# Issuing the background loads of an encoder kernel from ScalarE's queue

## The chip, the cores and the metric

The kernel runs on one core of a Trainium2 chip. The metric is the device time of one execution in microseconds; the time before is the median of three runs. One further execution was recorded by the hardware profiler, and all rows of the trace come from that one.

## The reference, cut to what matters

An encoder layer of width 1024 is applied to 512 prompt tokens and 2048 sample tokens, all in float32:

```python
h = rmsnorm(x, norm_pre)
z = h @ w_in
pool_u, pool_g, q, k, v, attn_g, merge = jnp.split(z, cuts, axis=-1)
pooled = multiscale_pool(pool_u)
pb = jnp.einsum('bsgc,gcd->bsgd', pooled, w_pool_group).reshape(B, S, POOL_WIDTH)
pb = pb * pool_scale * jax.nn.silu(pool_g)
q, k = rope(q, pos), rope(k, pos)
ab = windowed_attention(q, k, v, attn_sink) * jax.nn.silu(attn_g)
gates = jax.nn.sigmoid(merge)
m = gate_pool * (pb @ w_pool_proj) + gate_attn * (ab @ w_attn_proj)
out = x + rmsnorm(m @ w_out, norm_post)
```

## The kernel before, in words

Every float32 operand is split into a rounded high part and a low remainder (`hi_lo`, lines 106 to 108: ScalarE (ACT) copies the high part, VectorE (DVE) subtracts it), and every product takes three matmuls (`mm3`, lines 144 to 147). The kernel has two phases.

Phase 1 (`phase1`, to about 1180 us) forms the input projection in three blocks of 768, 896 and 896 tokens (`BLOCKS`). In each block, 26 pairs of weight columns go through a seven-product Strassen scheme (`pair_steps`, order M1, M6, M2, M5, M7, M3, M4). One product, an item, is 12 matmuls on a weight tile `w` that ACT and DVE have split; seven such tiles are in flight (`TILES = 7`). Between the items the results leave PSUM: ACT copies M1 (line 460) and M2 (`post.first`, lines 499 and 513), DVE adds the others (lines 464, 474, 442). M2 is accumulated on M1's bank, two items later, so the ACT copy of M1 must be done by then. The raw weights `R`, `A21` and the stored sums `Q` come by DMA on SyncE's queue (SP), in lines 402, 406 and 414.

Beside these, phase 1 runs background tasks, each a load and, later in the program, a form step (`task`):

- `stats_load` (line 253) loads rows of x for the next block, and ACT squares them (line 260): 28 loads.
- `later_load` (line 355) loads the transposed x of the next block, `later_form` normalizes it on DVE (line 367) and stores pieces `t` from GpSimd's queue (POOL): 32 loads.
- `late_load` (lines 679 and 680) loads back parts of the pooling branch put aside in block 0, `late_pool` finishes them (ACT's sigmoid in line 688) and stores `pb`: 20 loads.
- `split_load` (line 849) loads halves of `w_attn_proj`, `split_form` splits them on ACT and DVE and stores both parts: 16 loads in phase 1. Phase 2 uses the same function for other weights.
- `fold` multiplies the pooling groups into the pooling columns of w_in; `raw_load` (line 181) brings its operands, items 0 to 3 at the start and items 4 to 7 (12 loads) from about 113 us on. Its results go to memory as `wpool`.

All of these loads write tiles of one tag, `h` (`htile`), of which there are four buffers. The temporaries of the forms, the tiles of the stores `t`, `v`, `wpool`, `w_ap` and `pb`, and the operand pieces fetched in line 384 take buffers of the same tag, in turn. A load may go out when the former owner of its buffer is done with it, which for stored tiles means that the store has landed.

Phase 2 (from about 1180 us) is attention, the two branch projections and the output projection. None of its loads is touched.

The order on TensorE (PE) is the program's own. On the other engines and queues the framework lays down one fixed order in advance, by the order of the program and by when it reckons that an instruction can start; on the chip each engine then works strictly in that order, and a wait holds all that is behind it.

```python
        def raw_load(src, n):
            raw = (htile, utile)[n % 2 if n < 4 else 0]()
            nc.sync.dma_start(raw, src)
            return raw
```

Of the kernel before, what the change touches and what calls it, by code (L numbers as in the profile page):

```python
# [47 lines left out]
def encoder(ctx, tc, a, out):  # L48
    nc = tc.nc
    V, A, G, T = nc.vector, nc.scalar, nc.gpsimd, nc.tensor  # L50
# [8 lines left out]
    def psum(tag):  # L59
        return ps.tile([128, 512], F32, tag=tag, bufs=PS[tag], name="ps_" + tag)  # L60
# [4 lines left out]
    def htile():  # L65
        return sb.tile([128, 512], F32, tag="h", bufs=NH, name="h")
# [22 lines left out]
    def wtile():  # L89
        return sb.tile([128, 2, 512], F32R, tag="w", bufs=NW, name="w")  # L90

    def load(shape, src, tag):
        t = const.tile(shape, F32, tag=tag, name=tag)
        nc.sync.dma_start(t, src)
        return t
# [4 lines left out]
    def store(dst, src):  # L100
        G.dma_start(dst.bitcast(F32), src.bitcast(F32))

    def scratch(name, shape, dt=F32):
        return dr.tile(shape, dt, tag=name, bufs=1, name=name)

    def hi_lo(hi, lo, src):
        A.copy(hi, src)  # L107
        V.tensor_sub(lo, src, hi.bitcast(F32))  # L108
# [17 lines left out]
    rawu = [scratch(f"rawu{f}", [128, n0 + 24]) for f in range(8)]  # L126
    rawg = [scratch(f"rawg{f}", [128, n0]) for f in range(8)]
# [16 lines left out]
    def mm3(o, xs, ys, start, stop, more=False):  # L144
        T.matmul(o, lhsT=xs[0], rhs=ys[0], start=start, stop=False, skip_group_check=more)  # L145
        T.matmul(o, lhsT=xs[0], rhs=ys[1], start=False, stop=False, skip_group_check=more)  # L146
        T.matmul(o, lhsT=xs[1], rhs=ys[0], start=False, stop=stop, skip_group_check=more)  # L147
# [28 lines left out]
    def fold():  # L176
        steps, fetches = [], []

        def raw_load(src, n):
            raw = (htile, utile)[n % 2 if n < 4 else 0]()  # L180
            nc.sync.dma_start(raw, src)
            return raw

        def split(raw):
            w = wtile()
            hi_lo(w[:, 0, :], w[:, 1, :], raw)
            return w

        for g in range(4):
            for half in range(2):  # L190
                hs = slice(half * 512, (half + 1) * 512)
                n, raws = 2 * g + half, []

                def fetch(g=g, hs=hs, n=n, raws=raws):
                    raws += [raw_load(x, n) for x in (a["w_pool_group"][g], a["wu_t"][2 * g, :, hs], a["wu_t"][2 * g + 1, :, hs])]

                def make(n=n, raws=raws, fetch=fetch):
                    if n < 4:
                        fetch()
                    return [split(x) for x in raws]  # L200
                fetches.append(fetch)
                it = Item(make, 3)
                st = {}
                for i in range(4):
                    def f(it=it, st=st, i=i, g=g, half=half):
                        if i % 2 == 0:
                            st["p"] = psum("t")
                        o = st["p"][:, i % 2 * 256:(i % 2 + 1) * 256]
                        for c in range(2):
                            u = [it.w[1 + c][:, e, i * 128:(i + 1) * 128] for e in range(2)]  # L210
                            mm3(o, u, [it.w[0][:, e, c * 256:(c + 1) * 256] for e in range(2)], c == 0, c == 1)
                        if i % 2 == 1:
                            t = htile()
                            A.copy(t, st["p"])
                            tv = t.rearrange("p (r c) -> p r c", r=2)
                            k0 = half * 4 + i - 1
                            for c in range(2):
                                dst = wp[2 * g + c][:, k0 * 128:(k0 + 2) * 128].rearrange("p (r c) -> p r c", r=2)
                                store(dst, tv[:, :, c * 128:(c + 1) * 128])
                    steps.append((it, f))  # L220
        return steps, fetches
# [24 lines left out]
    def stats_load(s, ts):  # L246
        if s not in ssqs:
            ssqs[s] = sb.tile([128, 16], F32, tag="ssq", bufs=2, name="ssq")
        res = []
        for t in ts:  # L250
            for j in range(2):
                res.append((t, j, htile()))
                nc.sync.dma_start(res[-1][2], a["x"][t * 128:(t + 1) * 128, j * 512:(j + 1) * 512])
        return res

    def stats_sum(s, xs):
# [91 lines left out]
    def later_load(s, k, c):  # L348

        a_, b = BLOCKS[s]  # L350
        w = (b - a_) // 2
        res = []
        for j in range(2):
            t = htile()[:, 0:w].rearrange("p (i t) -> p i t", i=2)
            nc.sync.dma_start(t, a["xt"][k + 4 * j, :, a_:b].rearrange("p (i t) -> p i t", i=2)[:, :, c * w // 2:(c + 1) * w // 2])
            res.append(t)
        return res

# [317 lines left out]
    def late_load(f, j):  # L676
        m0, m1, g0, g1 = LATE[j][:4]
        u, g = htile(), htile()
        nc.sync.dma_start(u[:, 0:m1 - m0 + 16], rawu[f][:, m0:m1 + 16])
        nc.sync.dma_start(g[:, 0:g1 - g0], rawg[f][:, g0:g1])  # L680
        return u, g

    def late_pool(f, j, ug):
# [11 lines left out]
    def phase1():  # L695
# [29 lines left out]
        def src(i):  # L725
            return [(0, 2048, a["w_h"][i])]
# [6 lines left out]
        for s in range(len(BLOCKS)):  # L733
            specs = [(0, src(0), Rope(s, kd)), (1, src(1), Values(s))]
            for kv in range(NKV):
                g = {
                    "q": (2 + kv, src(2 + kv), Rope(s, qd[kv])),
                    "ag": (6 + kv, src(6 + kv), Silu(s, (2 * kv, 2 * kv + 1))),
                    "ga": (10 + kv, src(10 + kv), Gate(s, gad, (2 * kv, 2 * kv + 1))),
                    "gp": (14 + kv, src(14 + kv), Gate(s, gpd, (2 * kv, 2 * kv + 1))),  # L740
                }
# [19 lines left out]
        def hook(s, i, j, f):  # L761
            hooks.setdefault((s, i, j), []).append(f)
# [4 lines left out]
        def task(s, load, form):  # L767
            box = {}
            tasks[s].append((lambda: box.update(x=load()), lambda: form(box["x"])))

        for s in range(len(BLOCKS)):
            hook(s, 1, 6, lambda s=s: load_rope(s, "rope_q"))
            for (i, j), f in zip(((2, 2), (2, 4), (3, 0), (3, 3)), posts[NPAIR * s + 1].tr_steps()):
                hook(s, i, j, f)
            if s + 1 == len(BLOCKS):
                continue
            t0, t1 = BLOCKS[s + 1][0] // 128, BLOCKS[s + 1][1] // 128
            for t in range(t0, t1, 2):
                ts = range(t, min(t + 2, t1))

                def stats(x, s=s, last=t + 2 >= t1):
                    stats_sum(s + 1, x)
                    if last:
                        rstd(s + 1)
                task(s, lambda s=s, ts=ts: stats_load(s + 1, ts), stats)
            for k in range(4):
                for c in range(2):
                    def form(x, s=s, k=k, c=c):
                        if k + c == 0:
                            prep_r(s + 1)  # L790
                        later_form(s + 1, k, c, x)
                    task(s, lambda s=s, k=k, c=c: later_load(s + 1, k, c), form)
            hook(s, NPAIR - 3, 6, lambda s=s: fetch_operand(s + 1, XOP[ORDER[0]]))
            for j, r in enumerate(ORDER):
                hook(s, NPAIR - 1, j, lambda r=r: put_operand(XOP[r]))
                if j < 6:
                    hook(s, NPAIR - 1, j, lambda s=s, r=ORDER[j + 1]: fetch_operand(s + 1, XOP[r]))

        for i in range(2 * NLATE):
            f, j = i // 2, i % 2  # L800
            task(1 if i < LATE1 else 2, lambda f=f, j=j: late_load(f, j), lambda x, f=f, j=j: late_pool(f, j, x))
        ap_keys = [k for k in swp if k[0] == "w_ap"]
        for u in range(0, 16, 2):
            task(2, lambda u=u: [split_load(k) for k in ap_keys[u:u + 2]], lambda x: [split_form(*y) for y in x])
        hook(0, 3, 0, lambda: nc.sync.dma_start(cst["mask"], a["mask"]))
        for j in range(5):
            hook(0, 1, j, form_next)
# [7 lines left out]
        for s in range(len(BLOCKS)):  # L815
# [9 lines left out]
            n = len(tasks[s])  # L825
            for k, (begin, form) in enumerate(tasks[s]):
                t = t0 + (t1 - t0) * k / n
# [14 lines left out]
                    prog.append((None, fold_raws[i + 1]))  # L842
        return prog

    def split_load(key):

        h = htile()
        n, u, j = key
        nc.sync.dma_start(h, a[n][u, j] if n == "w_out" else a[n][u, :, j * 512:(j + 1) * 512])
        return h, swp[key]  # L850

    def split_form(h, dst):
        t = htile()
        hi, lo = t.bitcast(F32R), h.bitcast(F32R)
        hi_lo(hi, lo, h)
        for e, x in enumerate((hi, lo)):
            store(dst[:, e, :], x)
# [419 lines left out]
```

## Time and profile before

| | |
|---|---|
| runs | 2423.81, 2428.3, 2431.71 us; median 2428.3 |
| profiled execution | 2437.32 us, of which the span from first to last instruction is 2435.5 us |
| granted TensorE clock, mean | 0.983 of full speed |
| busy over the span | PE 96%, DVE 73%, ACT 47%, POOL 19% |

Two levels of time are seen here: the device time of a run, and the span in the trace, which is 1.8 us shorter than the device time of the same execution. The busy shares are means over two phases with different work, so the stretch from 60 to 1180 us, in which all loads of the change lie, has to be read by itself. "SPq" is SyncE's DMA queue; waits put down to it are times in which its next DMA was held.

### The profile page before, as it was taken

Reading aid. Unit: us, or ns where it says so; the run is one execution under the profiler, and the core shown is the slowest. Engines: PE = TensorE matmul, PEld = TensorE weight load, DVE = VectorE, ACT = ScalarE, POOL = GpSimd, SP = SyncE. Lnnn points to the kernel's source line nnn. Section 1 sums busy time; section 2 is a strip of 40 time slices with the busy share of each in tenths; the row PEclk is TensorE's granted clock in tenths of the full one; section 3 lists DMA queues with packets and bytes.
Section 4 is the critical chain, followed back from the end, with each engine's and each line's share of the span. In section 5 each row is a group of like instructions: output and inputs, shape, how many; then the busy total and the mean of one; then the engine's idle time right before and its main releaser. Section 6 shows DMA issues by size and latency. Waiting matters only on the chain.

```text
span 2435.5 us, 34771 instructions
## 1 busy us (share of the span) xinstructions
PE 2328.3 (96%) x11680; PEld 2070.4 (85%) x11680; DVE 1770.1 (73%) x3451; ACT 1149.8 (47%) x2511; POOL 458.4 (19%) x962
## 2 busy tenths in 40 slices
PE   5999999999999999999999889999999999999998
PEld 5899999898998999988899767787788788888887
DVE  7967789875777687777667667895788478578632
ACT  6355443545434345434443356674566366456411
POOL 2232233221222110323211111111110111021011
PEclk8999999999999999999999999999999999999999
DMA  6587786767577556757755597889788788877784
GB/s 234 184 274 248 253 276 224 280 212 236 182 236 245 163 172 243 250 201 257 258 170 171 194 318 224 267 254 319 274 268 265 271 262 251 278 261 239 258 290 174
DMA packets 197043, 586.83 MB, mean 241 GB/s; under 512 B 27265, under 2 KB 46209, under 8 KB 186881
## 3 DMA queue, kind: packets, MB, share of 16 engines
q1 hardware_dynamic: 152288, 406.26, 51.5%
q0 software_dynamic: 44576, 178.36, 19.9%
q8 instruction: 92, 1.51, 0.3%
q14 instruction: 87, 0.70, 0.1%
HBM read 406.19 MB, written 178.32 MB: 240 GB/s over the span
## 4 chain that ended last, share of the span: by engine, by line
PE 38%; DMA 5%; DVE 4%; ACT 2%; issue 1%; POOL 0%; SPq 0%; POOLq 0%; ACTq 0%; DVEq 0%
PE ps_g L146 6%; PE ps_g L145 6%; PE ps_g L147 6%; PE ps_t L1115 3%; PE ps_s L147 2%; PE ps_s L145 2%; PE ps_s L146 2%; DMA h<-pb 2%; PE ps_o L1131 2%; PE ps_o L1130 2%; DMA h<-ab 2%; PE ps_s L1083 2%; PE ps_s L1084 2%; DVE ps_s L1089 1%; DVE Q L108 1%
## 5 line engine op out<-in xcount | busy, mean ns | idle before, releaser
L145 PE MATMUL ps_g<-arena,w 128*128 128x512 f32 (+2 forms) x1264 | 494.6, 391 | 15.2 <-ACT arena L107 7.5
L146 PE MATMUL ps_g<-arena,w 128*128 128x512 f32 (+2 forms) x1264 | 479.2, 379 | 0.5 <-DVE arena L108 0.5
L147 PE MATMUL ps_g<-arena,w 128*128 128x512 f32 (+2 forms) x1264 | 477.8, 378 | 0.1
L145 PE MATMUL ps_s<-arena,w 128*128 128x448 f32 (+1 forms) x1248 | 448.7, 360 | 24.2 <-DVE u L474 9.3
L146 PE MATMUL ps_s<-arena,w 128*128 128x448 f32 (+1 forms) x1248 | 447.2, 358 | 3.2 <-DVE arena L108 3.1
L147 PE MATMUL ps_s<-arena,w 128*128 128x448 f32 (+1 forms) x1248 | 446.5, 358 | 1.5 <-DVE w L108 1.4
L107 ACT CAST w<-Q 128x512 fp32r<-128x512 f32 x312 | 190.1, 618 | 237.9 <-PE ps_s L147 177.8
L145 PEld LDWEIGHTS ps_g<-arena,w 128*128 128x128 f32 x1264 | 240.8, 190 | 38.0 <-ACT arena L107 10.3
L145 PEld LDWEIGHTS ps_s<-arena,w 128*128 128x128 f32 x1248 | 236.5, 190 | 42.6 <-DVE z L442 7.4
L147 PEld LDWEIGHTS ps_g<-arena,w 128*128 128x128 f32 x1264 | 240.2, 190 | 35.6 <-DVE w L108 0.4
L146 PEld LDWEIGHTS ps_g<-arena,w 128*128 128x128 f32 x1264 | 241.2, 191 | 21.8 <-DVE arena L108 2.6
L146 PEld LDWEIGHTS ps_s<-arena,w 128*128 128x128 f32 x1248 | 236.4, 189 | 17.7 <-DVE arena L108 5.6
L147 PEld LDWEIGHTS ps_s<-arena,w 128*128 128x128 f32 x1248 | 236.8, 190 | 15.1 <-DVE w L108 2.9
L108 DVE TENSOR_TENSOR w<-Q,w 128x512 fp32r<-128x512 f32 x312 | 212.4, 688 | 36.8 <-ACT w L107 32.1
L1091 ACT ACTIVATE R<-ps_s,nm 128x384 f32<-128x384 f32 (+1 forms) x320 | 179.7, 562 | 108.6 <-DVE nm L1089 99.5
L108 DVE TENSOR_TENSOR w<-R,w 128x512 fp32r<-128x512 f32 x234 | 160.6, 689 | 84.6 <-ACT w L107 82.9
L1089 DVE CUSTOM_DVE_ANT_0 ps_s<-ps_s,mask,nsink 128x384 f32<-128x384 f32 (+1 forms) x320 | 188.6, 593 | 17.3 <-PE ps_s L1084 15.7
L107 ACT CAST w<-R 128x512 fp32r<-128x512 f32 x234 | 143.7, 620 | 93.9 <-PE ps_s L147 48.9
L108 DVE TENSOR_TENSOR Q<-ps_t,Q 128x512 fp32r<-128x512 f32 x224 | 153.6, 689 | 38.9 <-ACT Q L107 36.1
L108 DVE TENSOR_TENSOR arena<-h,arena 128x512 fp32r<-128x512 f32 (+2 forms) x140 | 89.9, 658 | 107.8 <-ACT arena L107 107.2
L1115 PE MATMUL ps_t<-ident,R 128*128 128x128 f32 x896 | 140.3, 278 | 19.7 <-DVE R L1100 10.8
L107 ACT CAST Q<-ps_t 128x512 fp32r<-128x512 f32 x224 | 130.8, 584 | 44.7 <-PE ps_t L1115 22.0
(226 smaller groups left out, 4154.6 us busy)
## 6 DMA issues: line engine op xcount, KB each, us to landing
Q<-sw SPq DMA_DIRECT2D x52, 1024.0 KB, 6.0
R<-in_w_h SPq DMA_DIRECT2D x54, 768.0 KB, 6.0
w<-w_ap SPq DMA_DIRECT2D x80, 512.0 KB, 4.8
w<-w_pp SPq DMA_DIRECT2D x64, 512.0 KB, 5.4
w<-w_out SPq DMA_DIRECT2D x56, 512.0 KB, 4.9
sw<-Q POOLq DMA_DIRECT2D x26, 1024.0 KB, 5.7
arena<-q SPq DMA_DIRECT2D x20, 1024.0 KB, 7.4
q<-z POOLq DMA_DIRECT2D x128, 112.0 KB, 2.7
```

What stands on the lines that cost most here:

```text
L107: A.copy(hi, src)
L108: V.tensor_sub(lo, src, hi.bitcast(F32))
L145: T.matmul(o, lhsT=xs[0], rhs=ys[0], start=start, stop=False, skip_group_check=more)
L146: T.matmul(o, lhsT=xs[0], rhs=ys[1], start=False, stop=False, skip_group_check=more)
L147: T.matmul(o, lhsT=xs[1], rhs=ys[0], start=False, stop=stop, skip_group_check=more)
L1083: T.matmul(s, lhsT=q, rhs=st["kh"][:, kc], start=True, stop=False)
L1084: T.matmul(s, lhsT=q, rhs=st["kl"][:, kc], start=False, stop=True)
L1089: V.tensor_tensor_reduce(s, s, mask[:, kb0 * 128:kb1 * 128], -1.0, nsink[:, H:H + 1], ALU.add, ALU.min, nm[:, h:h + 1])
L1091: A.activation(P[:, 0:nk], s, AF.Exp, bias=nm[:, h:h + 1], scale=-1.0, accum_out=l[:, h:h + 1])
L1115: T.transpose(tp[:, h * 128:(h + 1) * 128], pr[h][:, i * 128:(i + 1) * 128], cst["ident"])
L1130: T.matmul(o, lhsT=v, rhs=pts[i][:, 0, :], start=i == 0, stop=False)
L1131: T.matmul(o, lhsT=v, rhs=pts[i][:, 1, :], start=False, stop=i == kb1 - kb0 - 1)
```

## The change

Five `dma_start` calls go from `nc.sync` to `A`, which is `nc.scalar`: the loads of fold items 4 to 7, of `stats_load`, `later_load` and `late_load`, and those of `split_load` where a background task calls it. What is loaded, the buffers and the order in the program stay.

```diff
         def raw_load(src, n):
             raw = (htile, utile)[n % 2 if n < 4 else 0]()
-            nc.sync.dma_start(raw, src)
+            (A if n >= 4 else nc.sync).dma_start(raw, src)
             return raw
...
                 res.append((t, j, htile()))
-                nc.sync.dma_start(res[-1][2], a["x"][t * 128:(t + 1) * 128, j * 512:(j + 1) * 512])
+                A.dma_start(res[-1][2], a["x"][t * 128:(t + 1) * 128, j * 512:(j + 1) * 512])
...
             t = htile()[:, 0:w].rearrange("p (i t) -> p i t", i=2)
-            nc.sync.dma_start(t, a["xt"][k + 4 * j, :, a_:b].rearrange("p (i t) -> p i t", i=2)[:, :, c * w // 2:(c + 1) * w // 2])
+            A.dma_start(t, a["xt"][k + 4 * j, :, a_:b].rearrange("p (i t) -> p i t", i=2)[:, :, c * w // 2:(c + 1) * w // 2])
...
         u, g = htile(), htile()
-        nc.sync.dma_start(u[:, 0:m1 - m0 + 16], rawu[f][:, m0:m1 + 16])
-        nc.sync.dma_start(g[:, 0:g1 - g0], rawg[f][:, g0:g1])
+        A.dma_start(u[:, 0:m1 - m0 + 16], rawu[f][:, m0:m1 + 16])
+        A.dma_start(g[:, 0:g1 - g0], rawg[f][:, g0:g1])
...
-            task(2, lambda u=u: [split_load(k) for k in ap_keys[u:u + 2]], lambda x: [split_form(*y) for y in x])
+            task(2, lambda u=u: [split_load(k, A) for k in ap_keys[u:u + 2]], lambda x: [split_form(*y) for y in x])
...
-    def split_load(key):
+    def split_load(key, queue=nc.sync):
...
-        nc.sync.dma_start(h, a[n][u, j] if n == "w_out" else a[n][u, :, j * 512:(j + 1) * 512])
+        queue.dma_start(h, a[n][u, j] if n == "w_out" else a[n][u, :, j * 512:(j + 1) * 512])
         return h, swp[key]
```

## Rows read from the trace of the kernel before

**Rows 1.** The profile's first part: busy us and share of the span, by engine.

```profile
PE 2328.3 (96%) x11680; PEld 2070.4 (85%) x11680; DVE 1770.1 (73%) x3451; ACT 1149.8 (47%) x2511; POOL 458.4 (19%) x962
```

**Rows 2.** Windows: stretch, length, busy us by engine, granted clock, DMA share, GB/s.

```profile
60.00:1180.00 1120.00, 1086.24 (x5635) 1023.27 (x5634) 852.94 (x1443) 484.81 (x894) 278.62 (x524) 0.99 0.68 232
860.00:1080.00 220.00, 220.00 (x1088) 202.10 (x1087) 170.16 (x275) 97.54 (x176) 45.63 (x93) 1.00 0.62 212
1080.00:1180.00 100.00, 93.26 (x454) 85.77 (x453) 66.18 (x109) 42.22 (x75) 31.97 (x63) 0.98 0.80 275
```

**Rows 3.** Waits of PE, 60 to 1180 us: us in total, times, longest us.

```profile
PE ps_s L145 <- DVE u L474: 7.0, 5, 2.7
PE ps_s L145 <- DVE z L442: 6.4, 3, 2.5
PE ps_t L145 <- ACT w L107: 5.2, 2, 4.5
PE ps_g L145 <- ACT s L460: 3.6, 1, 3.6
...
PE ps_t L581 <- DVE h L108: 0.4, 1, 0.4
```

**Rows 4.** Waits of SyncE's DMA queue, 60 to 1180 us.

```profile
SPq L402 <- DVE w L108: 213.9, 48, 28.9
...
SPq L355 <- DMA t<-h: 78.2, 23, 13.0
...
SPq L849 <- DMA w_ap<-h: 37.2, 12, 8.6
...
SPq L253 <- ACT h L260: 19.7, 12, 4.1
...
SPq L849 <- DVE w L108: 0.2, 1, 0.2
```

**Rows 5.** Issue of the loads in lines 355 and 679: ns min/median/max, first and last start.

```profile
L355 SPq DMA_DIRECT2D h<-in_xt x32: 367/378/517, 208.5 to 733.4; - x32
L355 SPq EVENT_SEMAPHORE  x30: 17/284/10552, 207.9 to 732.5; - x30
...
L679 SPq DMA_DIRECT2D h<-rawu  x10: 319/320/388, 744.7 to 1068.1; - x10
```

**Rows 6.** Waits of ACT that a DMA ended, 60 to 1180 us.

```profile
ACT h L107 <- DMA h<-in_w_ap: 27.1, 7, 5.1
ACT h L688 <- DMA h<-rawg: 25.9, 7, 10.6
...
ACT h L107 <- DMA w_ap<-h: 8.9, 4, 3.5
...
ACT w L107 <- DMA Q<-sw: 7.6, 4, 4.5
ACT w L107 <- DMA R<-in_w_h: 6.6, 2, 5.5
...
ACT h L688 <- DMA v<-h: 5.1, 1, 5.1
...
ACT h L107 <- DMA pb<-h: 3.4, 1, 3.4
...
ACT L533 <- DMA q<-z: 0.3, 1, 0.3
```

**Rows 7.** The same waits of ACT, 860 to 1080 us alone.

```profile
ACT h L688 <- DMA h<-rawg: 11.2, 4, 4.9
...
ACT z L499 <- DMA k<-z: 0.9, 1, 0.9
```

**Rows 8.** Timeline near 746 us: start, us, engine, what; in brackets the idle time before.

```profile
749.98 0.53 ACT L688 ACTIVATE h<-h 128x392 f32<-128x392 f32 x1 [10.60 <-DMA h<-rawg]
...
741.61 0.69 DVE L367 SCALAR_TENSOR_TENSOR h<-h,gpre,rbc 128x448 f32<-128x448 f32 x1 [6.67 <-DMA h<-in_xt]
...
746.02 0.47 PE L145 MATMUL ps_s<-arena,w 128*128 128x448 f32 x1 [2.55 <-DVE z L442]
```

## The prediction

> **What bounds the kernel now.** I read the busy shares first, then the stretch in which the change acts, then the waits of PE in it, and last the waits of the queues and of ACT. PE is busy for 2328.3 of 2435.5 us, 96% [rows 1]: TensorE is the bound, and all that another engine or queue can give or take is PE's idle time. All loads that the change moves start between 113 and 1180 us, so I cut out 60 to 1180 us. There PE is busy for 1086.24 of 1120 us, idle for 33.8 [rows 2]. This is the whole purse: no relief in this stretch can give back more than 33.8 us, 1.4% of the time. The ten rows of PE's waits there sum to 33.5 us, from 7.0 down to 0.4 [rows 3], and none names a DMA: PE waits for evictions by DVE and ACT, and for two weight tiles in the fold (5.2 us). A late load reaches PE only through ACT or DVE standing still.
>
> How well does PE bear a standing ACT? In 60 to 1180 us ACT waits 156.9 us for DMAs (15 rows, 27.1 down to 0.3 [rows 6]). In 860 to 1080 us it waits 31.3 us for them (six rows, 11.2 down to 0.9 [rows 7]) and PE loses nothing, 220.00 of 220 us [rows 2]. In 1080 to 1180 us, where the loads of w_attn_proj lie, it waits 39.4 us for those loads and for stores that give back `h` buffers (27.1, 8.9 and 3.4 [rows 6]; all three fall in this stretch), and PE loses 6.74 of 100 us [rows 2]. So one us of ACT standing costs PE between 0 and 6.74 / 39.4 = 0.17 us. I take 0.17 as the price, since that stretch holds the very loads in question.
>
> **The change part by part.** It moves 108 loads: 12 of the fold, 28 of x, 32 of transposed x, 20 of the late pooling, 16 of w_attn_proj. No byte, buffer or compute instruction is added or taken.
>
> *Issue.* On SP one issue takes 320 ns (line 679) to 378 ns (line 355) [rows 5]; 108 of them are 35 to 41 us, I take 37, off SP and onto ACT. ACT has no DMA issue in this trace. ACT is idle for 635 of 1120 us [rows 2], and that idle time is the cover. The ends for PE are 0 and 37 × 0.17 = 6 us; I take 2, because most of these loads will stand in front of an ACT instruction that has to wait anyway. If the cover were gone, the 37 us would be paid at up to one for one.
>
> *Waits for a buffer.* A load is held until its `h` buffer is free. On SP, the six lines moved were held for 291 us in this stretch (30 rows, 78.2 down to 0.2 [rows 4]), 52 of these holds, 192 us, ending with the landing of a store. This is what moves to ACT, and behind it stand the casts of weight tiles and the copies of M1 and M2 that PE needs. The ends are 0 (ACT comes to each load after its buffer is free) and 291 us. SP has little else to do and arrives early, so its holds overstate ACT's. The nearest row is ACT's own use of such buffers: of 26 allocations of an `h` tile that ACT writes first (16 in the split of w_attn_proj, 10 in the late pooling), six waited for a store, 8.9 + 3.4 + 5.1 = 17.4 us [rows 6], 0.67 us for each. The 28 loads of x are mostly freed by ACT's own squares (19.7 us of SP's holds [rows 4]), which ACT itself has done before, so they cost nothing. That leaves 80 loads × 0.67 = 54 us. Half of it I count as spent already: near 746 us ACT stood for 10.60 us in front of the sigmoid, because the load that it waited for was itself held for a buffer [rows 8]. With the load on ACT, the wait moves to the load and the wait for the landing shrinks. So 27 us are new, × 0.17 = 4.6 us. The ends are 0 and 291 × 0.17 = 49 us.
>
> *What it gives.* On SP, weight loads in lines 402, 406 and 414 no longer stand behind a held background load. What those weights cost now is small: ACT waited 6.6 us for R and 7.6 us for Q [rows 6], 14.2 × 0.17 = 2.4 us for PE; I take 3 with the few DVE waits of the kind. SP's own holds in line 402, 213.9 us [rows 4], are waits for R buffers to come free, and stay. The ends are 0 and 11 us (worked out under the first rival).
>
> The row with the longest hold shows the mechanism: before a load in line 355 the queue's semaphore instruction lasted up to 10552 ns [rows 5], and the next DMA of that queue came after. The Trainium skill, page "DMA: Bandwidth & Descriptors", section "Anatomy of one DMA", says that a DMA's semaphore wait is done by the issuing sequencer before dispatch, not by the DMA engines; this row agrees, and taken with all of SP's holds it would give the upper end, about 2428 + 49 = 2477 us.
>
> *Sum.* 2 + 4.6 − 3 = +3.6 us. The profiled execution took 2437.32 us, span 2435.5 and 1.8 around it, and would become 2440.9; it stands 9 us above the median of the three runs, so I put the same +3.6 on that: 2428.3 + 3.6 = **2432 us**. A change under 0.3% (7.3 us) cannot be told from none here. My forecast is therefore no change that can be told, with a lean to slower; its own range is 2421 to 2436.
>
> **The rivals.**
> *Faster: the background loads stop queueing on SP.* In the SP order a background load also stands behind held weight loads, and lands late; the consumers then stand, DVE for 6.67 us near 742 us, after which PE lost 2.55 us [rows 8]. If the loads go out sooner, PE can win back 2.55 us here, the 5.2 us of the fold's weight tiles and the 3.6 us in front of the copy of M1 [rows 3]: 11 us, so 2417 us. For it: SP is held for 213.9 us in line 402 [rows 4]. Against it: the 291 us of holds are at the loads themselves, which had reached the head of their queue, so a buffer and not the queue was what they lacked.
>
> *Slower: ACT held in front of a PSUM copy.* The place is a load that ACT reaches before its buffer is free, with the copy of M1 (line 460) or a cast behind it. The single wait of 3.6 us for that copy [rows 3] came right after ACT had waited 3.4 us for a store to free a buffer [rows 6]. PE does one item between M1 and M2, and the wait decides once ACT is held longer than that item lasts. Without the halving and without cover, 54 + 37 = 91 us × 0.17 = 15 us: 2443 us. For it: 52 of SP's holds ended with a store, 3.7 us each on average. Against it: ACT stood 10.60 us near 746 us and PE's loss there is put down to DVE [rows 8].
>
> *Much slower: all holds carried over*, 291 + 37 = 328 us × 0.17 = 56 us, 2484 us; ACT would have to reach every load as early as SP did, while most of its casts are paced by PE.
>
> *The change frees nothing on SP*: the loads keep the same gates and share the same DMA engines, whose mean share in this stretch is 0.68 [rows 2]. Then the credit of 3 us falls away, 2435 us. The Trainium skill, same page, section "Issuing engines are not separate DMA queues", says that DMAs interleave on the same engines whoever issues them and that only issue time is saved; nothing in this trace contradicts it, and the sum by it would be 2435 us, inside the forecast.
>
> **How the numbers follow.** The forecast of no telling change, with the last rival inside it, has 0.42; faster 0.25; slower at some 2443 us 0.28; much slower 0.05. Moving loads between queues also lays the orders of both queues down anew, which can shift single PE waits of 1 to 4 us [rows 3] either way, so I give the faster side its quarter though its mechanism is weakly borne out. The range goes from 2414, just past the faster rival, to 2456, between the two slower ones; that leaves out some 0.1 on each side.
>
> **What would show it.** In the changed kernel's profile: 108 DMA issues on ACT's queue, of 0.3 to 0.4 us; ACT waits at the moved lines that a store ended, 25 to 90 us in sum; the waits for landing in lines 688 and 107 smaller than before; PE's idle time in 60 to 1180 us between 30 and 42 us. The forecast is wrong to the slow side if PE's waits for the copies in lines 460 and 499 come to more than 10 us, and wrong to the fast side if PE's idle time there falls under 27 us. If the time moves while PE's idle time in this stretch stays, the cause is not one that I name.

## The result and the profile after

The changed kernel takes 2460.06 us, the median of six runs (2451.81 to 2471.18); the kernel before, run beside it, 2429.12 us (2423.81 to 2431.71, six runs). The ratio is 1.0123 [1.0099, 1.0147]: slower by 1.2%, some 31 us, and 4 us above the upper end of the range. The profiled execution of the changed kernel took 2455.05 us, with a span of 2453.3 us; the one before took 2437.32 us. The two traces that can be compared thus lie 17.7 us apart, and the rest of the 31 us is the place of each within its runs: the one before stood 8 us above its median, this one 5 us below.

The first part of the changed kernel's profile (compare [rows 1]):

```profile
PE 2326.8 (95%) x11680; PEld 2073.7 (85%) x11680; DVE 1768.3 (72%) x3451; ACT 1151.6 (47%) x2511; POOL 461.9 (19%) x962
```

No engine has more work. PE was busy 2328.3 us and is busy 2326.8; what was added is idle time. The same windows as in [rows 2], and two more that cut the stretch in halves:

```profile
60.00:1180.00 1120.00, 1066.67 (x5524) 1010.42 (x5524) 839.88 (x1423) 475.78 (x877) 276.58 (x515) 0.98 0.67 226
860.00:1080.00 220.00, 218.99 (x1100) 204.69 (x1099) 169.41 (x273) 99.34 (x176) 43.16 (x88) 1.00 0.63 213
1080.00:1180.00 100.00, 92.11 (x439) 84.17 (x438) 70.46 (x114) 40.69 (x71) 29.68 (x60) 0.97 0.72 241
...
60.00:740.00 680.00, 643.83 (x3449) 618.66 (x3449) 514.72 (x896) 290.96 (x554) 176.76 (x314) 0.97 0.69 233
740.00:1200.00 460.00, 437.46 (x2139) 404.48 (x2138) 333.78 (x543) 192.90 (x339) 104.71 (x210) 0.98 0.65 219
```

In 60 to 1180 us PE is idle for 53.3 us, where it was 33.8: 19.6 us more, which is all of the 17.7 us between the two profiled executions. In the two halves, the same windows of the kernel before read:

```profile
60.00:740.00 680.00, 656.80 (x3535) 630.53 (x3534) 524.32 (x914) 299.26 (x567) 179.19 (x321) 0.98 0.70 237
740.00:1200.00 460.00, 447.01 (x2188) 408.59 (x2187) 345.30 (x554) 194.90 (x344) 102.05 (x208) 1.00 0.66 224
```

PE loses 13.0 us more in the first half and 9.6 us more in the second. The stretch 1080 to 1180 us, from which the forecast took its price, lost 1.2 us more. The moved loads end near 1190 us; phase 1 itself does not end at 1180 us: its last additions come near 1390 us in the trace before and near 1415 us in this one. Who keeps PE waiting is in its waits, 60 to 1180 us, of the changed kernel (us in total, times, longest; twelve rows that sum to 53.2 us, against ten with 33.5):

```profile
PE ps_s L145 <- DVE u L474: 24.8, 10, 4.6
PE ps_s L145 <- DVE z L442: 6.7, 2, 3.9
PE ps_t L145 <- ACT w L107: 4.5, 2, 2.4
PE ps_g L145 <- ACT s L460: 3.8, 4, 2.3
PE ps_g L145 <- ACT w L107: 3.6, 1, 3.6
```

Beside [rows 3] one row has clearly grown: DVE's PSUM addition in line 474, from 7.0 to 24.8 us. The copy of M1 in line 460 cost PE 3.6 us and costs 3.8. Yet DVE has no more to do, so it must itself have been kept waiting: its longest row of waits, for ACT's casts of weight tiles, grew by 25.8 us (60 to 1200 us, before and then after):

```profile
DVE w L108 <- ACT w L107: 102.1, 76, 5.7
DVE w L108 <- ACT w L107: 127.9, 86, 9.1
```

The waits of ACT, 60 to 1200 us, of the changed kernel:

```profile
ACT w L107 <- DMA t<-h: 40.8, 5, 11.0
ACT h L260 <- DMA h<-in_x: 25.9, 10, 6.8
...
ACT h L688 <- DMA h<-rawg: 20.3, 8, 7.0
...
ACT h L107 <- DMA h<-in_w_ap: 15.7, 8, 5.1
...
ACT s L460 <- DMA w_ap<-h: 13.0, 3, 6.1
...
ACT w L107 <- DVE h L369: 8.3, 2, 4.3
ACT s L460 <- DMA v<-h: 8.2, 2, 4.6
...
ACT w L107 <- DMA pb<-h: 5.0, 1, 5.0
```

A cast of a weight tile (line 107) reads no tile of a store, and neither does the copy of M1. That a store `t<-h` ended 40.8 us of idle time in front of casts means that a load stood between: ACT was held at the load until that store gave back its `h` buffer, and the cast went next. Added up, ACT's waits that a store of an `h` tile ended were 17.4 us in six [rows 6] and are 86.3 us in 19. Waits that ended when DVE or POOL had read the `h` tile of a form, as in the row with line 369, come to 20.0 us more and are absent before. In turn the waits for the landing of the loads moved (x, `rawg`, `w_ap`, the fold's operands) shrank from 100.8 to 75.7 us.

The timeline of the changed kernel near 403 us shows the chain from the hold to PE (start, us, engine, what; in brackets the idle time before):

```profile
393.92 1.34 POOL L101 DMA_DIRECT2D t<-h  x2
...
402.13 0.97 ACTq L355 DMA_DIRECT2D h<-in_xt  x2
...
403.20 0.62 ACT L107 CAST w<-Q 128x512 fp32r<-128x512 f32 x1 [8.95 <-DMA t<-h]
...
403.86 0.69 DVE L108 TENSOR_TENSOR w<-Q,w 128x512 fp32r<-128x512 f32 x1 [4.18 <-ACT w L107]
...
409.07 0.55 DVE L474 TENSOR_TENSOR u<-ps_s,s 128x384 f32<-128x384 f32 x1
...
409.77 0.41 PE L145 MATMUL ps_s<-arena,w 128*128 128x384 f32 x1 [1.69 <-DVE u L474]
```

Two stores of `t` are issued from 393.92 on and land at 402.06 and 402.66. ACT's queue stands in front of the first load from 393.64 to 402.09; ACT, through with its last cast at 394.25, sends the two loads from 402.13 on and computes again at 403.20. DVE stands for 4.18 us in front of the low part of that weight tile, then works through what has piled up, and its addition for PE comes at 409.07, too late by 1.69 us. No instruction on this chain waits for the data of the load that ACT sent.

### The profile page after: what moved, and what is told of

Same layout as the page of the kernel before. It is cut to its first block, busy times and chain, and to the rows that moved or that the text cites. A ratio compares the mean times of both kernels' runs of the same rounds, so it can differ in the third digit from the quotient of the medians.

```text
span 2453.3 us, 34691 instructions
## 1 busy us (share of the span) xinstructions
PE 2326.8 (95%) x11680; PEld 2073.7 (85%) x11680; DVE 1768.3 (72%) x3451; ACT 1151.6 (47%) x2511; POOL 461.9 (19%) x962
## 3 DMA queue, kind: packets, MB, share of 16 engines
q0 software_dynamic: 44576, 178.36, 19.6%
## 4 chain that ended last, share of the span: by engine, by line
PE 39%; DMA 4%; DVE 4%; issue 2%; ACT 2%; POOL 1%; SPq 0%; POOLq 0%; ACTq 0%; DVEq 0%
PE ps_g L146 6%; PE ps_g L145 6%; PE ps_g L147 6%; PE ps_t L1115 3%; PE ps_s L145 3%; PE ps_s L147 3%; PE ps_s L146 3%; DMA h<-ab 2%; PE ps_o L1131 2%; PE ps_o L1130 2%; PE ps_s L1084 1%; PE ps_s L1083 1%; DVE ps_s L1089 1%; DVE Q L108 1%; DMA h<-pb 1%
## 5 line engine op out<-in xcount | busy, mean ns | idle before, releaser
L145 PE MATMUL ps_s<-arena,w 128*128 128x448 f32 (+1 forms) x1248 | 452.1, 362 | 44.1 <-DVE u L474 29.8
L145 PEld LDWEIGHTS ps_s<-arena,w 128*128 128x128 f32 x1248 | 239.0, 192 | 62.8 <-issue 19.5
L146 PEld LDWEIGHTS ps_s<-arena,w 128*128 128x128 f32 x1248 | 239.3, 192 | 17.1 <-DVE arena L108 6.4
L147 PEld LDWEIGHTS ps_s<-arena,w 128*128 128x128 f32 x1248 | 239.7, 192 | 15.0 <-DVE w L108 3.8
```

## The experiments

Three theories were set against each other. H (hold): ACT, held in order at loads whose buffer a store has yet to free, delays DVE and then PE. I (issue): what costs is the issuing itself, 108 DMA instructions of 0.33 to 0.37 us each on an engine that computes. O (order): what costs is the order of ACT's and DVE's instructions, which the framework lays down anew whenever loads leave SyncE's queue, whatever is held.

**Parts alone.** Each kernel moves some of the loads of the diff and leaves the rest on SP. The kernel before, run beside them, took 2431.95 us.

```diff
 # the part with transposed x only (32 loads)
-            nc.sync.dma_start(t, a["xt"][k + 4 * j, :, a_:b]...)
+            A.dma_start(t, a["xt"][k + 4 * j, :, a_:b]...)
 # the part with x and the fold only (28 and 12 loads)
-            nc.sync.dma_start(raw, src)
+            (A if n >= 4 else nc.sync).dma_start(raw, src)
-                nc.sync.dma_start(res[-1][2], a["x"]...)
+                A.dma_start(res[-1][2], a["x"]...)
 # the part with the late pooling and w_attn_proj only (20 and 16 loads)
-        nc.sync.dma_start(u[:, 0:m1 - m0 + 16], rawu[f]...)
+        A.dma_start(u[:, 0:m1 - m0 + 16], rawu[f]...)
...
-            task(2, lambda u=u: [split_load(k) for k in ap_keys[u:u + 2]], ...)
+            task(2, lambda u=u: [split_load(k, A) for k in ap_keys[u:u + 2]], ...)
...
```

Transposed x alone:

> Only the 32 loads of transposed x (line 355) go to ScalarE's queue; the other 76 stay on SyncE's. Theory H (holds: ACT, held at a load until a store has given the h buffer back, keeps the weight casts behind it, DVE's subtractions wait for them, and DVE's additions that free PE's banks stand behind those): in the changed kernel 40.8 us of ACT's holds ended with a store of t, the most of all, so this part alone should cost 10 to 20 of the 31 us, and rows of ACT waiting for t should be there with 25 to 50 us. Theory I (issue time on ACT): 32 of 108 issues, 32/108 of 31 = 9 us. Theory O (the new fixed order, whatever is held): no forecast of size, anywhere between 0 and 31 us.

x and the fold alone:

> Only the 28 loads of x (line 253) and the 12 of the later fold items (line 181) go to ScalarE's queue. Theory H: ACT's own squares free most of these buffers, and the holds for stores of v and wpool in the changed kernel come to 14.6 us there; 0 to 5 us slower. Theory I: 40 of 108 issues, 40/108 of 31 = 11 us slower. Theory O: anywhere between 0 and 31 us.

Late pooling and `w_attn_proj` alone:

> Only the 20 loads of the late pooling (lines 679, 680) and the 16 of w_attn_proj (line 849) go to ScalarE's queue. Theory H: holds that ended with stores of w_ap, pb and v come to some 30 us in the changed kernel; 8 to 18 us slower, the loss in 740 to 1200 us. Theory I: 36 of 108 issues, 10 us slower. Theory O: anywhere between 0 and 31 us. By theory H the three parts together make about the 31 us of the whole.

| moved to ACT | us | ratio to before | ACT held for stores, us (times), longest | PE waits 60 to 1200, us |
|---|---|---|---|---|
| nothing | 2431.95 | 1 | 17.4 (6), 5.1 | 36.0 |
| transposed x | 2443.32 | 1.0039 [1.0015, 1.0063] | 50.3 (12), 8.7 | 45.4 |
| x and fold | 2432.96 | 1.0005 [0.9988, 1.0022] | 27.5 (10), 4.9 | 39.4 |
| late pooling, `w_attn_proj` | 2441.17 | 1.0037 [1.0011, 1.0063] | 31.8 (10), 5.9 | 45.1 |
| all | 2460.06 | 1.0123 [1.0099, 1.0147] | 86.3 (19), 11.0 | 58.6 |

Forty loads, more than a third of all, cost nothing that can be told (the interval ends at 0.2%): those of x, many of whose buffers ACT's own squares free, and those of the fold. The other two parts cost 0.4% each, and each where its loads lie: with transposed x PE's busy time in 60 to 740 us falls from 656.80 to 649.05, with the late loads that in 740 to 1200 us from 447.01 to 439.40. The three parts sum to 0.8%, less than the whole and than the 31 us that H asked for, but each interval is about 0.2% wide on either side; that they do more together is not shown.

The medians lie 11.4, 1.0 and 9.2 us above the kernel before. The first and the third fit I (9 and 10 us) as well as H; only the second, where I asked for 11 us, tells them apart, and O named no size. The waits of PE are those of one execution each: in the seven kernels of this document whose times cannot be told from the kernel before (that one among them) they lie between 36.0 and 44.0 us, so 45.4 and 45.1 alone would show little.

**The issue without the hold.** The kernel before, with one small store more (8 KB) from ACT's queue right behind each copy of M1, that is, 78 issues at the place the slower rival named. Its data has just been made by ACT, so nothing holds it.

```diff
                         A.copy(st["s"], acc)
+                    A.dma_start(scratch(f"iss{pair.n}_{s}", [16, 128]), st["s"][0:16, 0:128])
```

> The kernel before, all its loads on SyncE's queue, plus one small store of 8 KB from ScalarE's queue behind the copy of M1 in each of the 78 pairs of phase 1. It waits for nothing but that copy, which is ACT's own, so ACT issues 78 DMAs and is not held. Theory H: 0 to 6 us slower. Theory I (issue time on ACT): 78 of 108 issues, some 22 us slower.

It took 2430.95 us beside 2432.1, ratio 1.0002 [0.9981, 1.0023]. The issues of this kernel (ns min/median/max, first and last start):

```profile
L461 ACTq DMA_DIRECT2D iss<-s x78: 308/309/914, 41.5 to 1350.4; - x78
```

24 us of issue time on ACT leave no mark on the time, where I asked for 22 us. Theory I is out as far as issue time goes.

**The hold without the issue.** The loads stay on SP, but ACT first writes one column of each of the 108 buffers. So ACT is held where it would be held at the load, and issues nothing. The loads on SP now wait for ACT's column as well, but the landing waits are no longer for it: ACT's for the moved loads are 83.6 us (100.8 before), DVE's for transposed x 26.5 us (25.7).

```diff
             t = htile()[:, 0:w].rearrange("p (i t) -> p i t", i=2)
+            A.copy(t[:, 0, 0:1], ones)
             nc.sync.dma_start(t, a["xt"][k + 4 * j, :, a_:b]...)
...
```

> All loads are issued from SyncE's queue as before, but ahead of each of the 108 ACT writes one column of the buffer, which the load then overwrites. ACT is held for the buffer just as in the changed kernel and issues no DMA. Theory H: as slow as the changed kernel, 2450 to 2475 us, with ACT holds that end with stores of 70 us or more. Theory I: 108 tiny copies of some 0.2 us cost next to nothing; 2425 to 2440 us. Theory O: the order is laid down anew here too, so 2425 to 2465 us, with no tie to the holds.

2446.96 us, ratio 1.0060 [1.0039, 1.0081]: slower by half as much as the change. H asked for 2450 us or more and I for 2440 or less, so both missed; O's 2425 to 2465 us holds it, as it would hold almost any result. The stretches tell more. Its windows and the longest rows of its ACT waits, first 60 to 740 us, then 740 to 1200 us (lines 358 and 856 are added copies):

```profile
60.00:740.00 680.00, 646.05 (x3467) 620.69 (x3466) 515.43 (x895) 297.52 (x625) 172.78 (x311) 0.98 0.68 231
740.00:1200.00 460.00, 446.92 (x2203) 414.69 (x2202) 348.12 (x566) 201.88 (x386) 107.74 (x216) 0.99 0.68 228
```

```profile
ACT h L358 <- DMA t<-h: 33.4, 10, 8.1
...
ACT h L856 <- DMA w_ap<-h: 6.1, 6, 1.5
```

| stretch | kernel | ACT held for stores, us (times), longest | PE waits, us |
|---|---|---|---|
| 60 to 740 | before | 0 | 23.0 |
| | changed | 40.8 (7), 9.6 | 36.0 |
| | ACT touches buffers | 50.5 (17), 8.1 | 33.5 |
| 740 to 1200 | before | 17.4 (6), 5.1 | 12.9 |
| | changed | 45.5 (12), 11.0 | 22.5 |
| | ACT touches buffers | 38.4 (21), 6.3 | 13.1 |

In the first stretch the holds sum to more than in the change and PE loses 10.5 of the change's 13 us, without one load on ACT. In the second they sum to nearly as much but are many and short (1.8 us each against 3.8), and PE loses nothing. So holds without an issue are enough for about half of the cost. That it is the long ones that cost is a guess from these two stretches, and the kernels under "More buffers" below speak against it.

**Another queue.** The same 108 loads from GpSimd's queue (POOL).

```diff
-            nc.sync.dma_start(t, a["xt"][k + 4 * j, :, a_:b]...)
+            G.dma_start(t, a["xt"][k + 4 * j, :, a_:b]...)
...
```

> The same 108 loads as in the change, issued from GpSimd's queue. ACT issues nothing and is not held; the holds go to GpSimd, behind which stand the stores. Theory H: ACT has no holds ended by stores beyond those of the kernel before, and the time is that of before within 10 us, 2422 to 2442 us. Theory O (any move off SyncE's queue lays down a new order, and that costs): about as slow as the change, 2450 us or more.

2475.89 us, ratio 1.0201 [1.0167, 1.0234]: the worst of all, where H expected no loss and O 2450 us or more. So leaving SyncE's queue can cost without ACT being held at a load, and H alone does not cover this kernel. Its issue row, a wait of PE and a wait of ACT, 60 to 1200 us:

```profile
L355 POOL DMA_DIRECT2D h<-in_xt x32: 709/725/743, 220.9 to 763.7; - x32
```

```profile
PE ps_t L145 <- ACT w L107: 14.4, 1, 14.4
```

```profile
ACT h L688 <- DMA h<-rawg: 54.0, 9, 13.2
```

ACT's waits that a store ended are 22.5 us in four here, little more than before. The loads now stand in order with POOL's stores, and ACT waits 54.0 us for `rawg` where it waited 25.9 [rows 6]; PE once stands 14.4 us for the fold's weights. PE's waits in the stretch, 60.4 us, explain some 24 of the 44 us lost. Much of the rest is in the matmuls themselves: PE is busy 10.1 us longer than before [rows 1] for the same 11680 of them, at a mean granted clock of 0.978 against 0.983 in the two profiled executions.

```profile
PE 2338.4 (94%) x11680; PEld 2076.7 (84%) x11680; DVE 1767.6 (71%) x3451; ACT 1145.6 (46%) x2511; POOL 524.1 (21%) x1070
```

**More buffers.** If the hold is the cause, more `h` buffers take the gap away. They need room, so one weight tile in flight is given up in all of these. With each number of buffers both versions run: the loads on SP (as before) and on ACT (as in the change).

```diff
-TILES = 7
+TILES = 6
...
-NW, NZ, NH, NR = 7, 6, 4, 3
+NW, NZ, NH, NR = 6, 6, 6, 3
```

Six buffers, SP and then ACT:

> The kernel before with six h buffers in place of four, paid for with one weight buffer less (NW 6, TILES 6). It is the base for the next run; 2425 to 2450 us.

> The changed kernel with six h buffers and six weight buffers, to be compared with the run before it. Theory H: with more buffers a load finds a free one more often, the holds of ACT that end with stores fall well under the 95 us of the changed kernel, and the gap to the run before it falls with them, to 0 to 15 us. Theories I and O: issues and queue are those of the change, so the gap stays about 30 us.

Four buffers, the control for the lost weight tile, SP and then ACT:

> The kernel before with six weight buffers and the four h buffers that it has: the base that the run with six h buffers lacked. 2425 to 2445 us.

> The changed kernel with six weight buffers and four h buffers. If the two more h buffers closed the gap (theory H), it is open here: 20 to 40 us above the run before it, with 70 us or more of ACT holds. If it was the sixth weight buffer's loss, or the order that came with it, that closed the gap, it is closed here too, under 10 us.

Five buffers, SP and then ACT:

> The kernel before with six weight buffers and five h buffers: 2425 to 2445 us.

> The changed kernel with six weight buffers and five h buffers. Theory H: the gap to the run before it lies between those with four and with six h buffers, 5 to 25 us, and so do the holds. Another theory has no reason for a gap that falls with the number of h buffers.

| `h` buffers | on SP: us, ratio to before | on ACT: us, ratio to before | gap, us | ACT held for stores: SP, ACT |
|---|---|---|---|---|
| 4 | 2437.57, 1.0028 [1.0008, 1.0048] | 2459.54, 1.0123 [1.0093, 1.0153] | 22.0 | 11.5 in 7, 71.9 in 25 |
| 5 | 2432.16, 0.9999 [0.9980, 1.0019] | 2436.04, 1.0019 [0.9999, 1.0039] | 3.9 | 6.0 in 3, 42.9 in 15 |
| 6 | 2428.84, 0.9984 [0.9962, 1.0005] | 2434.08, 1.0004 [0.9985, 1.0024] | 5.2 | 18.6, 17.1 in 8 |

ACT's longest waits for a store, 60 to 1200 us, in the ACT version with four buffers, then with six:

```profile
ACT w L107 <- DMA t<-h: 26.7, 4, 12.6
```

```profile
ACT h L107 <- DMA w_ap<-h: 4.4, 1, 4.4
ACT s L460 <- DMA pb<-h: 3.7, 1, 3.7
```

With four buffers the gap is 22 us; one buffer more takes it down to 3.9, which with intervals of 0.2% on both versions (some 7 us on the gap) cannot be told from nothing; H had asked for 5 to 25. The loads, their queue and their issues are the same in all three, so this also excludes that the issuing queue costs the 22 us by itself. It speaks against O too: set against its partner on SP, the five-buffer ACT version has 54 of ACT's 2511 and 137 of DVE's 3451 compute instructions in another place of the order, the four-buffer one 36 and 92, the change itself 47 and 114. The part with transposed x, 11 us slower than the kernel before, moves only 4 and 59. A new order of the change's extent is there without the gap; that one particular order costs some of it is not excluded.

The five-buffer kernel still holds ACT for 42.9 us: the sum of the holds is no fixed price. Nor is their length. The windows with four buffers, on ACT and then on SP:

```profile
60.00:740.00 680.00, 650.09 (x3511) 625.90 (x3511) 526.18 (x917) 297.14 (x565) 179.43 (x320) 0.98 0.69 235
740.00:1200.00 460.00, 435.71 (x2109) 399.74 (x2108) 334.57 (x539) 191.59 (x336) 100.25 (x204) 0.98 0.65 219
```

```profile
60.00:740.00 680.00, 653.45 (x3528) 627.64 (x3527) 527.14 (x919) 300.47 (x568) 181.01 (x322) 0.99 0.69 236
740.00:1200.00 460.00, 447.65 (x2202) 415.78 (x2200) 344.54 (x554) 195.84 (x346) 100.83 (x207) 0.99 0.66 227
```

In the first stretch the ACT version is held for stores for 39.6 us in ten waits, the longest 12.6, and PE is idle for only 3.4 us more than on SP. In the second the holds are shorter, 32.4 us in 15, the longest 5.5, and PE is idle for 11.9 us more. What makes a hold dear was not found. None of the versions is told apart from the kernel before on the fast side; the nearest is six buffers with the loads on SP.

## Why the prediction was wrong

**The bound and the place were right.** It set out from PE's idle time in 60 to 1180 us, and there the difference lies. It put that idle time between 30 and 42 us; it came to 53.3. It asked for ACT waits of 25 to 90 us that a store ended, and they were 86.3 (60 to 1200 us). ACT's moved loads take 0.33 to 0.37 us to issue, as read from SP.

**Issue, +2 us: nothing.** The direction of the argument was right (most of it is covered), and 78 issues gave 1.0002.

**Waits for a buffer, +4.6 us: the step that failed,** at both factors, and at the price more than at the count.

- The count. It took 0.67 us for each of 80 loads, from tiles that ACT itself writes in a form, and called half of the 54 us already spent, 27 us new. Measured, 69 us of ACT's waits for stores are new (86.3 − 17.4), and landing waits gave back 25.1 of them: some 44 us against 27, and 64 with the 20.0 us that DVE or POOL ended. A likely reason is that a form comes late, when its data has landed, and a load early, when its buffer is still with a store. SP's own holds at these loads (291 us, [rows 4]) were far too high an end. That the x loads cost nothing proved right.
- The price. 0.17 is a mean over 1080 to 1180 us, where ACT stood mostly before casts of `w_attn_proj` itself. PE's waits grew by 22.6 us (58.6 − 36.0, 60 to 1200 us): 0.5 for one of the 44 us, 0.35 for one of the 64. The prediction had a single wait at a far higher price before it, 3.4 us of ACT and right behind it 3.6 us of PE, and still took the mean. And there is no fixed price at all: in the kernel in which ACT touches the buffers 38.4 us of holds cost nothing, with five buffers 42.9 us next to nothing, and with four buffers the longer holds cost less than the shorter ones. What decides the price stays open.

**Relief of SP, −3 us: nothing.** ACT waited 14.2 us for the tiles R and Q [rows 6], and now 14.5. SP is held longer in line 402, for R buffers:

```profile
SPq L402 <- DVE w L108: 313.0, 50, 27.9
```

That was 213.9 us [rows 4]; lines 414 and 406 are held for 96.5 and 73.0 us longer by the same kind of wait. The rival by which the change frees nothing on SP was right as to this term: of the 291 us that SP no longer stands at the moved loads, it stands 269 us more at these three lines.

**The rivals.** The slower one, 2443 us, had the cause, ACT held in order at a load, and too small a size: 91 us × 0.17. Of its place only half was right. The copy of M1 is held at times, 13.0 and 8.2 us of ACT's waits, but PE's wait for it rose by 0.2 us only. Where the chain was followed, the loss goes the longer way round that the prediction did not follow: cast, DVE's low part, DVE's additions queued behind it, PE. At the copy itself the timeline of the changed kernel near 1110 us shows a detour with one more link:

```profile
1107.94 3.05 ACTq L849 DMA_DIRECT2D h<-in_w_ap  x2
...
1111.04 0.53 ACT L460 COPY s<-ps_g 128x448 f32<-128x448 f32 x1 [3.86 <-DMA w_ap<-h]
...
1112.12 0.69 DVE L108 TENSOR_TENSOR w<-R,w 128x512 fp32r<-128x512 f32 x1 [3.92 <-ACT w L107]
...
1115.17 0.62 ACT L107 CAST h<-h 128x512 fp32r<-128x512 f32 x1 [3.08 <-DMA h<-in_w_ap]
...
1115.82 0.69 DVE L108 TENSOR_TENSOR h<-h 128x512 fp32r<-128x512 f32 x1 [3.00 <-ACT h L107]
...
1116.43 0.61 DVE L442 TENSOR_TENSOR z<-ps_s,u 128x448 f32<-128x448 f32 x1
...
1117.10 0.47 PE L145 MATMUL ps_s<-arena,w 128*128 128x448 f32 x1 [2.80 <-DVE z L442]
```

ACT copies M1 after 3.86 us of standing, and then casts the next weight tile, for which DVE has stood 3.92 us. DVE then stands 3.00 us more, for the cast of a half of `w_attn_proj`, whose load ACT had sent only at 1107.94 and which landed at 1115.07. Behind that come DVE's addition and PE's loss of 2.80 us. Here, then, the last link is a late landing and not a hold. The prediction's own test for the slow side, more than 10 us of PE's waits at the copies, would therefore have missed the loss; the row to watch was that of line 474.

The much slower rival's 328 us did not come: ACT reaches the loads later than SP did, as argued against it. The faster rival's gain did not show either: DVE's waits for landings in line 367 went from 25.7 to 33.3 us.

The rule cited from the Trainium skill, page "DMA: Bandwidth & Descriptors", section "Anatomy of one DMA — SWDGE (gpsimd) path", that the issuing sequencer does a DMA's semaphore wait, agrees with the changed kernel, where that instruction in front of the loads of line 355 lasts up to 8448 ns on ACT's queue (the hold near 403 us above):

```profile
L355 ACTq DMA_DIRECT2D h<-in_xt x32: 374/374/607, 217.6 to 746.5; - x32
L355 ACTq EVENT_SEMAPHORE  x25: 17/128/8448, 217.5 to 746.0; - x25
```

The other rule cited from the Trainium skill, same page, section "Issuing engines are not separate DMA queues", that only issue time is saved by spreading DMAs over engines, agrees on the side of the gain: ACT's waits for R and Q did not fall (14.2 us, then 14.5). What the kernel lost lies outside it.

**A term that the prediction did not have: the clock.** In the changed kernel's trace PE falls to the lower of its two clock levels (1.2 GHz) 11 times between 60 and 1200 us, nine of them within some 2 us of the end of a wait of PE of 2.1 to 5.0 us; in the trace before six times, five of them so after a wait of 1.8 to 3.6 us. So a wait of PE can be paid a second time. Near 224 us PE waited 4.56 us for line 474; the next six microseconds and the six behind them (granted clock 0.50, then 0.99):

```profile
224.00:230.00 6.00, 5.89 (x18) 5.92 (x19) 6.00 (x9) 3.09 (x5) 4.58 (x9) 0.50 0.43 119
230.00:236.00 6.00, 6.00 (x36) 6.00 (x36) 5.95 (x13) 3.21 (x6) 4.40 (x10) 0.99 0.83 260
```

**What stays open.** The chain was followed at single places; how much of the 22.6 us goes which way is not shown, though the row of line 474 alone rose by 20.5 us (9.3 to 29.8, 60 to 1200 us). And one profiled execution of each kernel shows 17.7 us, where the medians lie 31 us apart. Counted by work, the trace shows more: PE runs the same matmuls in the same order in both, and those that the kernel before runs from 60 to 1200 us take the changed one 26.5 us longer, 22.6 us by idle time (17.3 for the work that stood before 740 us, 5.3 for the work behind) and 4.0 us by slower matmuls. Behind them it gains 6.7 us back, before them it was 2.2 us ahead. The clock is a likely part of the rest: the six runs of the changed kernel have a mean granted clock of 0.980 to 0.982 (median 0.981), the kernel before in the later comparisons a median of 0.984 or 0.985. By an estimate from PE's 2328 us of busy time that is 7 to 10 us, of which the two profiled executions (0.982 and 0.983) can show some 2 us. That the holds lower the clock between runs was not tested.

## What to carry to other kernels

A load whose buffer is still with a store holds the queue that issues it, with the issuing engine's compute behind it, so be slow to issue it from an engine whose later work feeds the bound; SyncE was held for 291 us at these loads [rows 4] in the faster kernel. Loads whose buffers the issuing engine frees itself are the ones to move, if any (here the part with them cost nothing that could be told), and where others must, one more buffer is the remedy to try first (here a gap of 22 us became 3.9). Do not price holds by a mean share of the idle time: here neither their sum nor their length set the loss, so try the move on the chip, part by part.

## What the runs showed of the hardware that was not expected

A DMA issue occupied ACT's queue for 0.31 to 0.37 us (medians by line), and 78 of them cost nothing that can be measured, behind the very copies that PE depends on. The same load of line 355 took 0.374 us to issue on ACT and 0.378 us on SP [rows 5], but 0.725 us on POOL. And a wait of 4.56 us was followed by six microseconds in which PE ran 18 matmuls in place of 36.
